# The w_down products of a hybrid mLSTM and attention block: factors without accumulating loads, gated factors split ahead, two-bank products

## The chip, the cores and the metric

One Trainium2 chip, one of its cores. The metric is the device time of one execution in microseconds: the median of several executions without the profiler. A profile is one further execution, taken with the profiler on; its own time stands beside its span below.

## What is computed

One block of a streaming encoder on 512 tokens of width 2048 in float32. A shared pre-normalised input feeds an mLSTM part and a differential attention part; their heads go through w_out and are added to x. The rest is a SwiGLU mixer, and this is the part that matters here:

```python
h2 = rmsnorm(x, norm2_g)                                   # 512 x 2048
x = x + (silu(h2 @ w_gate) * (h2 @ w_up)) @ w_down         # 5632 gated features
return rmsnorm(x, final_g)
```

w_gate and w_up are 2048 x 5632, w_down is 5632 x 2048. Every factor of a product is held as two numbers, hi (the value rounded to the matmul's format, `fp32r`) and lo (what is left), and each product is three matmuls: hi*hi, hi*lo and lo*hi.

## The kernel before

**Order of the stages.** In-projections, attention and mLSTM (to about 640 us of the profiled execution), w_out (to about 810 us), w_gate and w_up (810 to 1693 us), the w_down products (1693 to 2044 us), then a tail with what is left of w_down, the final norm and the stores.

**Gate and up.** `NFB` = 22 groups `g` of 256 features. Each runs `group` (L961) twice, for w_gate and then for w_up. A group multiplies by a block scheme with 7 products instead of 8 (names P1 to P7, in the order of `ORDER`), each product being 24 matmuls of 128x256 columns. Its weight factors come from the generator `left_factors` (L851), which loads blocks with SP, forms sums of blocks on DVE and splits each factor (`split`, L96: the hi cast on ACT at L98, the lo subtraction on DVE at L99). `factor` (L921) pulls factors `LAP` = 2 ahead of the product that uses them; whi and wlo have three buffers. `after` (L974) takes a product out of PSUM. At the end of the second group `up` (L1032) has the two gated tiles `C1` and `C2`. For g < 16 it forms seven combinations of their halves and POOL stores them to a DRAM tensor `actv`, in float32; for the last six groups POOL stores the tiles to `actd`.

**The w_down products (L1069).** The first 16 groups' rows of w_down are done in four row blocks (`ci`, 0 to 3) and two column halves (`dg`, 0 and 1), eight units `u` in all; each unit has seven products, in the order `DOWN`, and each product has 24 matmuls of 512 columns in two halves `h`. A product has three inputs:

- The weight factor. `load` (L885) fetches blocks of w_down with SP; for two of the five blocks of each `h` a second block is added in flight by an accumulating DMA that POOL issues (L891). Two more sums per `h` are formed on DVE (L913, L915). `upto` (L898) sets how many loads are issued ahead. The factor is then split at L98 and L99.
- The gated factor. `variant` (L946) loads one of the seven combinations for row block `ci` from `actv` with SP into a tile `ra` of two buffers (L952) and splits it on ACT and DVE into hi and lo tiles of the pool `A` (32 tiles). In the loop this happens during dg = 1, one variant per product, for the next row block; four are made in the last up group and three in unit 0.
- The sum so far. Each product is made anew in two PSUM banks (one of the pool `acc`, one of `aux`, four each), copied to a tile M by ACT in row block 0 (L1088), and added to M by DVE in the others (L1090), 512 columns at a time.

**The tail.** `combine` (L1097) turns the seven M tiles of a column half into blocks of the result on DVE, scales them on ACT, and POOL adds x1 from DRAM to them with an accumulating DMA. The last six feature groups are done in two chunks of four and two (`CHUNKS`) by `proj_tok` and the loop at L1212; `Gated` (L1125) loads and splits their activations, `last_weights` (L1166) loads and splits the last chunk's weights.

**What sets the order.** Each engine and each issuing queue (SP, POOL) works in its own fixed order and waits at the head of it. A planner puts the instructions into these orders when the kernel is built, following the program and tile reuse: a tile is given out again when its last reader is done, and the first writer of the new tile waits for that. So the SP queue stops at a load whose tile is still read, and ACT stops at a cast whose input has not landed.

Of the kernel before, what the change touches and what calls it, by code (L numbers as in the profile page):

```python
# [30 lines left out]
def build(nc, tc, ctx, a, out):  # L31
# [11 lines left out]
    pacc = pool("acc", 4, space=bass.MemoryType.PSUM)  # L43
    paux = pool("aux", 4, space=bass.MemoryType.PSUM)
# [23 lines left out]
    def tacc():  # L68
        return pacc.tile([128, 512], F32, tag="acc", name=nm("acc"))

    def taux():
        return paux.tile([128, 512], F32, tag="aux", name=nm("aux"))
# [763 lines left out]
    actd = dram.tile([NFB, 2, 128, 512], F32, name="actd")  # L836
    actv = dram.tile([4 * NSP, 7, 128, 256], F32, name="actv")
# [7 lines left out]
    DOWN = ["P1", "P3", "P6", "P5", "P7", "P4", "P2"]  # L845
# [5 lines left out]
    def left_factors():  # L851
# [33 lines left out]
        def load(u, h, i, ring):  # L885
            j, n, j2, n2 = ((0, 0, 0, 0), (1, 1, 1, 1), (0, 0, 0, 1), (1, 1, 0, 1), (1, 0, 1, 0))[i]
            ci, dg = divmod(u, 2)
            t = ring()
            nc.sync.dma_start(t, a["w_ds"][ci, dg, j, n, h])
            if (j, n) != (j2, n2):  # L890
                G.dma_start(t, a["w_ds"][ci, dg, j2, n2, h], accum_op=ALU.add)  # L891
            return t

        order = [(u, i, h) for u in range(2 * NSP) for i in range(5) for h in range(2)]
# [3 lines left out]
        def upto(k):  # L898
            while pos[0] < min(k, len(order)):
                u, i, h = order[pos[0]]  # L900
                got[u, i, h] = load(u, h, i, tR if h and (u, i) != (0, 0) else lambda: tW("raw", bufs=7))
                pos[0] += 1

        upto(2)
        for u in range(2 * NSP):
            k = 10 * u
            for pi, name in enumerate(DOWN):
                if u or pi:
                    upto(k + (14 if pi == 0 else 16 if pi < 6 else 20))
                for h in range(2):  # L910
                    B11, B22, T1, T3, B21 = (got.get((u, i, h)) for i in range(5))
                    if name == "P6":
                        V.tensor_tensor(B22, B22, T1, ALU.add)  # L913
                    if name == "P4":
                        V.tensor_tensor(B22, B22, B21, ALU.add)  # L915
                    yield parts({"P1": B11, "P3": B22, "P6": B22, "P5": T1, "P7": T3, "P4": B22, "P2": B21}[name])
# [28 lines left out]

    def variant(ci, name, into):  # L946

        v = ["P1", "P7", "P2", "P4", "P5", "P6", "P3"].index(name)
        into[name] = []
        for h in range(2):  # L950
            if more:
                r = more[2].tile([128, 512], F32, tag="ra", name=nm("ra"), bufs=2)  # L952
            else:
                r = tW("raw", bufs=7)[:, 0:512]
            g0 = 4 * ci + 2 * h
            nc.sync.dma_start(r.rearrange("p (g c) -> p g c", g=2), actv[g0:g0 + 2, v].rearrange("g p c -> p g c"))
            hi, lo = tA(), tA()
            split(hi, lo, r)
            into[name].append((hi, lo))

    def group(scale, done, first=False, last=False):  # L961
# [12 lines left out]
        def after(name):  # L974
            if name == "P1":
# [48 lines left out]
    for g in range(NFB):  # L1024
# [7 lines left out]
        def up(i, t):  # L1032
            V.tensor_tensor(t, t, sl[i], ALU.mult)
            if g >= 4 * NSP:
                G.dma_start(actd[g, i], t)
                return
# [10 lines left out]
            for k, t in ((0, C1), (2, C2), (4, Sa)):  # L1047
                G.dma_start(actv[g, k:k + 2].rearrange("v p c -> p v c"), t.rearrange("p (v c) -> p v c", v=2))
            G.dma_start(actv[g, 6], Sb[:, L])

        group(None, gate, first=g == 0)
        group(None, up, last=g == NFB - 1)


    late[0].close()
    mst, (pM,) = stage(("mm", 1),)
    more.extend(stage(("rr", 1), ("ra", 1)))
    more[1:] = more[1]
    M = [{}, {}]

    def product_down(banks, w, name, h):
        for m in range(2):
            rs = slice(m * 512, m * 512 + 512)
            hi, lo = got_v[name][h]
            for tt in range(2):
                ts = slice(m * 256 + tt * 128, m * 256 + tt * 128 + 128)
                three(banks[tt], hi[:, ts], lo[:, ts], w[0][:, rs], w[1][:, rs], h == 0 and m == 0, h == 1 and m == 1)

    for u in range(2 * NSP):  # L1069
        ci, dg = divmod(u, 2)  # L1070
        got_v = cur_v
        if dg == 1:
            cur_v = {}
        for pi, name in enumerate(DOWN):
            if u == 0 and pi < 3:
                variant(0, DOWN[4 + pi], cur_v)
            if dg == 1 and ci + 1 < NSP:
                variant(ci + 1, name, cur_v)
            banks = [tacc(), taux()]
            for h in range(2):  # L1080
                product_down(banks, factor(), name, h)
            if ci == 0:
                M[dg][name] = pM.tile([128, 1024], F32, tag="M", name=nm("M"), bufs=14)
            t = M[dg][name]
            for tt in range(2):
                cs = slice(tt * 512, tt * 512 + 512)
                if ci == 0:
                    SC.copy(t[:, cs], banks[tt])  # L1088
                else:
                    V.tensor_tensor(t[:, cs], banks[tt], t[:, cs], ALU.add)  # L1090

    more[0].close()
# [4 lines left out]
    def combine(dg):  # L1097
# [12 lines left out]
        V.tensor_tensor(P6, P6, P1, ALU.add)  # L1110
        V.tensor_tensor(P7, P7, P6, ALU.add)
        V.tensor_tensor(P4, P4, P7, ALU.add)
        out_(P4, 1, 0)
        V.tensor_tensor(P3, P3, P5, ALU.add)
        V.tensor_tensor(P3, P3, P6, ALU.subtract)
        out_(P3, 0, 1)
# [210 lines left out]
```

## Time and profile before

| | us |
|---|---|
| median of 3 executions | 2181.36 |
| lowest and highest of them | 2181.03, 2182.97 |
| the profiled execution, its own time | 2190.05 |
| its span, first to last instruction | 2188.3 |
| span after the start of the w_down products | 495.1 |

The page of the profile gives each engine's busy time over the span; the stretches in the rows below give the same by stage. PE is TensorE's matmuls, PEld its weight loads, DVE VectorE, ACT ScalarE, POOL GpSimd, SP the queue that issues most DMAs. PEclk is the share of full clock that TensorE was granted: 1.00 is 2.4 GHz, 0.50 is 1.2 GHz. A matmul's printed duration covers its whole passage and is longer than the step from one to the next, so work is counted by the step between starts. Idle time stands in brackets behind an instruction with what ended it.

### The profile page before, as it was taken

How to read it: one execution, taken by the hardware profiler on the slowest of the kernel's cores; microseconds unless marked ns; L12 is line 12 of the kernel's file. 1: busy time of each engine (PE TensorE's matmuls, PEld its weight loads, DVE VectorE, ACT ScalarE, POOL GpSimd, SP SyncE). 2: the span in 40 equal slices, each digit the busy share in tenths (PEclk: the TensorE clock that was granted, in tenths of full speed). 3: DMA queues.
4: the chain of work that ended last, by engine and by line, in shares of the span. 5: the costliest groups of instructions: out<-in, count | busy, mean ns of one | idle time of the engine just before them, and what ended most of it. 6: DMA issues, size and time to landing. Idle time of an engine off the chain costs nothing.

```text
span 2188.3 us, 33437 instructions
## 1 busy us (share of the span) xinstructions
PE 2142.0 (98%) x13305; PEld 1938.2 (89%) x13305; DVE 1569.6 (72%) x2362; ACT 992.7 (45%) x1515; POOL 133.8 (6%) x189
## 2 busy tenths in 40 slices
PE   9999999999999999999999999999999799999998
PEld 7888889988888889999999999999999577778786
DVE  6267776366544468888888888888889467779745
ACT  6256675355434354344344443343444454444423
POOL 0011110000000000000000000000000000001100
PEclk9999999999999999999999999999999999999999
DMA  6232112332234424343443434433335986876732
GB/s 257 96 96 78 62 53 72 116 97 87 82 112 146 140 92 131 124 145 119 129 135 119 137 121 133 131 123 117 121 121 168 284 228 184 242 210 156 203 106 77
DMA packets 100749, 292.56 MB, mean 134 GB/s; under 512 B 10976, under 2 KB 27376, under 8 KB 100592
## 3 DMA queue, kind: packets, MB, share of 16 engines
q1 hardware_dynamic: 86832, 247.42, 34.5%
q0 software_dynamic: 13760, 43.00, 8.4%
q8 instruction: 104, 1.70, 0.3%
q14 instruction: 53, 0.43, 0.1%
HBM read 264.16 MB, written 26.22 MB: 133 GB/s over the span
## 4 chain that ended last, share of the span: by engine, by line
PE 85%; DMA 6%; DVE 6%; ACT 2%; issue 1%; ACTq 0%; POOL 0%; DVEq 0%; SPq 0%; POOLq 0%
PE acc L159 9%; PE acc L158 9%; PE acc L160 9%; PE acc L933 8%; PE acc L932 8%; PE acc L931 8%; PE aux L933 6%; PE aux L932 6%; PE aux L931 6%; DMA ra<-actv 4%; PE acc L189 4%; PE acc L190 4%; PE acc L191 4%; DVE wlo L99 2%; PE aux L160 1%
## 5 line engine op out<-in xcount | busy, mean ns | idle before, releaser
L98 ACT CAST whi<-raw 128x1024 fp32r<-128x1024 f32 (+2 forms) x573 | 593.6, 1037 | 807.4 <-PE acc L932 238.8
L99 DVE TENSOR_TENSOR wlo<-raw,whi 128x1024 fp32r<-128x1024 f32 (+2 forms) x573 | 690.5, 1206 | 305.8 <-ACT whi L98 295.0
L158 PE MATMUL acc<-whi,A 128*128 128x512 f32 (+1 forms) x1056 | 404.0, 384 | 21.4 <-ACT whi L98 18.2
L159 PE MATMUL acc<-wlo,A 128*128 128x512 f32 (+1 forms) x1056 | 403.7, 382 | 9.5 <-DVE wlo L99 9.5
L160 PE MATMUL acc<-whi,A 128*128 128x512 f32 (+1 forms) x1056 | 400.7, 379 | 0.0
L158 PEld LDWEIGHTS acc<-whi,A 128*128 128x128 f32 x1056 | 200.0, 190 | 59.4 <-ACT whi L98 22.5
L159 PEld LDWEIGHTS acc<-wlo,A 128*128 128x128 f32 x1056 | 200.3, 190 | 48.0 <-DVE wlo L99 15.0
L160 PEld LDWEIGHTS acc<-whi,A 128*128 128x128 f32 x1056 | 200.4, 190 | 34.0
L932 PE MATMUL acc<-A,whi 128*128 128x256 f32 x704 | 199.3, 283 | 0.5 <-DVE A L99 0.5
L931 PE MATMUL acc<-A,whi 128*128 128x256 f32 x704 | 199.4, 283 | 0.0
L931 PE MATMUL acc<-h,whi 128*128 128x256 f32 x704 | 199.4, 283 | 0.0
L933 PE MATMUL acc<-h,wlo 128*128 128x256 f32 x704 | 199.2, 283 | 0.0
L932 PE MATMUL acc<-h,whi 128*128 128x256 f32 x704 | 199.2, 283 | 0.0
L933 PE MATMUL acc<-A,wlo 128*128 128x256 f32 x704 | 199.2, 283 | 0.0
L933 PE MATMUL aux<-h,wlo 128*128 128x256 f32 x528 | 149.7, 284 | 0.8 <-DVE wlo L99 0.8
L931 PE MATMUL aux<-h,whi 128*128 128x256 f32 x528 | 149.6, 283 | 0.6 <-ACT whi L98 0.6
L189 PE MATMUL acc<-A,whi 128*128 128x512 f32 x384 | 150.1, 391 | 0.0
L190 PE MATMUL acc<-A,whi 128*128 128x512 f32 x384 | 149.8, 390 | 0.0
L191 PE MATMUL acc<-A,wlo 128*128 128x512 f32 x384 | 149.8, 390 | 0.0
L933 PE MATMUL aux<-A,wlo 128*128 128x256 f32 x528 | 149.4, 283 | 0.0
L931 PE MATMUL aux<-A,whi 128*128 128x256 f32 x528 | 149.4, 283 | 0.0
L932 PE MATMUL aux<-A,whi 128*128 128x256 f32 x528 | 149.4, 283 | 0.0
(280 smaller groups left out, 4123.9 us busy)
## 6 DMA issues: line engine op xcount, KB each, us to landing
raw<-in_w_g_dram SPq DMA_DIRECT2D x88, 512.0 KB, 3.5
raw<-in_w_u_dram SPq DMA_DIRECT2D x88, 512.0 KB, 3.6
raw<-in_w_ds_dram SPq DMA_DIRECT2D x80, 512.0 KB, 5.1
raw<-in_w_aqk_dram SPq DMA_DIRECT2D x32, 512.0 KB, 3.4
raw<-in_w_o_dram SPq DMA_DIRECT2D x32, 512.0 KB, 3.5
raw<-in_w_ds_dram POOLq DMA_DIRECT2D x32, 512.0 KB, 8.2
raw<-in_w_b_dram SPq DMA_DIRECT2D x31, 512.0 KB, 4.0
actv<-x POOLq DMA_DIRECT2D x48, 256.0 KB, 3.4
```

What stands on the lines that cost most here:

```text
L98: SC.copy(hi, src)
L99: V.tensor_tensor(lo, src, hi.bitcast(F32), ALU.subtract)
L158: PE.matmul(acc, lh, rh, start=first, stop=False)
L159: PE.matmul(acc, lh, rl, start=False, stop=False)
L160: PE.matmul(acc, ll, rh, start=False, stop=last)
L189: PE.matmul(banks[f], wh[:, cs], xh[k], start=first, stop=False)
L190: PE.matmul(banks[f], wh[:, cs], xl[k], start=False, stop=False)
L191: PE.matmul(banks[f], wl[:, cs], xh[k], start=False, stop=last)
L931: PE.matmul(bank, w[0][:, cs], hi, start=m == 0, stop=False)
L932: PE.matmul(bank, w[0][:, cs], lo, start=False, stop=False)
L933: PE.matmul(bank, w[1][:, cs], hi, start=False, stop=m == 7)
```

## The change

Four things are changed, all in or around the w_down products.

1. *Weight factors.* The block scheme's order is now P1, P5, P3, P7, P2, P6, P4, and each unit loads its four blocks per `h` once, all with SP. The accumulating DMAs are gone; the four sums per `h` that the scheme needs are formed on DVE in place.
2. *Gated factors.* They are split where they are made. `up` queues calls (`later`) that split each tile, hi into a new tile x and lo in place, and POOL stores both halves; `after` runs one of them behind the products P1, P6, P7 and P2 of the next group. `variant` then is four loads per product straight into hi and lo tiles, with no work on ACT or DVE. The pool of these tiles grows from 32 to 38 (`tAA`), and the table `NEXT` says at which product of which half the next row block's variants are loaded. The last six groups' activations (`actd`, `Gated`) are treated likewise, and the first chunk of them takes the place of a fifth row block in `NEXT`.
3. *PSUM.* Until the end of gate and up it is `acc` and `aux` as before. In the w_down products P1 of each column half has two banks of its own and gathers all four row blocks there, never copied to M; the other six products share two pairs of banks, and are taken out by one instruction over 1024 columns. In the tail `acc` has four banks where the pairs were.
4. *Tail.* `combine` is a generator in four steps, one at each of the first two granules of every column block; `last_weights` yields once more, between a load and its splits.

```diff
+    def tAA():
+        nAA[0] += 1
+        if (nAA[0] - 1) % 38 < 32:
+            return tA()
+        return more_a[0].tile([128, 512], F32R, tag="aa", name=nm("aa"))
...
-        def load(u, h, i, ring):
-            j, n, j2, n2 = ((0, 0, 0, 0), (1, 1, 1, 1), (0, 0, 0, 1), (1, 1, 0, 1), (1, 0, 1, 0))[i]
-            ci, dg = divmod(u, 2)
-            t = ring()
-            nc.sync.dma_start(t, a["w_ds"][ci, dg, j, n, h])
-            if (j, n) != (j2, n2):
-                G.dma_start(t, a["w_ds"][ci, dg, j2, n2, h], accum_op=ALU.add)
+        def load(u, i, h):
+            j, n = ((0, 0), (0, 1), (1, 1), (1, 0))[i]
+            t = tR() if (h if u else i > 1) else tW("raw", bufs=7)
+            nc.sync.dma_start(t, a["w_ds"][u // 2, u % 2, j, n, h])
...
-        upto(2)
+        upto(4)
...
-                    upto(k + (14 if pi == 0 else 16 if pi < 6 else 20))
+                    upto(8 * u + (8, 8, 8, 10, 10, 12, 14)[pi])
...
+                    t, o = {"P1": (B11, None), "P5": (B11, B12), "P3": (B22, None), "P7": (B12, B22),
+                            "P2": (B21, None), "P6": (B11, B22), "P4": (B21, B11)}[name]
+                    if o is not None:
+                        V.tensor_tensor(t, t, o, ALU.add)
+                    yield parts(t)
...
     def variant(ci, name, into):
...
-            nc.sync.dma_start(r.rearrange("p (g c) -> p g c", g=2), actv[g0:g0 + 2, v].rearrange("g p c -> p g c"))
-            hi, lo = tA(), tA()
-            split(hi, lo, r)
-            into[name].append((hi, lo))
+            into[name].append((tAA(), tAA()))
+            for p in range(2):
+                nc.sync.dma_start(into[name][h][p].bitcast(F32), actv[p, v, 2 * ci + h])
...
         def after(name):
+            if later and name in ("P1", "P6", "P7", "P2"):
+                later.pop(0)()
...
+            def halves(t):
+                hi, lo = tX(F32R)[:, :t.shape[1]], t.bitcast(F32R)
+                split(hi, lo, t)
+                return hi, lo
...
+            def keep(k, t, g=g, cs=cs):
+                for p, r in enumerate(halves(t)):
+                    r = r.bitcast(F32)
+                    if k == 6:
+                        G.dma_start(actv[p, 6, g // 2, :, cs], r)
+                    else:
+                        G.dma_start(actv[p, k:k + 2, g // 2, :, cs].rearrange("v p c -> p v c"),
+                                    r.rearrange("p (v c) -> p v c", v=2))
+            later.extend(partial(keep, k, t) for k, t in ((0, C1), (2, C2), (4, Sa), (6, Sb[:, L])))
...
+    psum[0].close()
+    pst, (pP1,) = banks_of(("p1", 2))
+    psum[:] = banks_of(("pair", 2))
+    NEXT = {(0, 3): 0, (0, 5): 1, (1, 1): 2, (1, 2): 3, (1, 3): 4, (1, 4): 5, (1, 5): 6}
...
+            nxt = NEXT.get((dg, pi))
+            if nxt is not None:
+                if ci + 1 < NSP:
+                    variant(ci + 1, DOWN[nxt], cur_v[1])
+                elif nxt < CHUNKS[0]:
+                    chunks[0].more(tAA)
+            if name == "P1":
+                if ci == 0:
+                    M[dg][name] = pP1.tile([128, 1024], F32, tag="p1", name=nm("p1"))
+                bank, fresh_, done_ = M[dg][name], ci == 0, ci == NSP - 1
+            else:
+                bank, fresh_, done_ = psum[1][0].tile([128, 1024], F32, tag="pair", name=nm("pair")), True, True
...
-                if ci == 0:
-                    SC.copy(t[:, cs], banks[tt])
-                else:
-                    V.tensor_tensor(t[:, cs], banks[tt], t[:, cs], ALU.add)
+                SC.copy(M[dg][name], bank)
+            else:
+                V.tensor_tensor(M[dg][name], bank, M[dg][name], ALU.add)
```

## Rows read from the trace of the kernel before

**Rows 1.** The page, section 1: PE's busy time, share, instructions.

```profile
PE 2142.0 (98%) x13305; PEld 1938.2 (89%) x13305; DVE 1569.6 (72%) x2362; ACT 992.7 (45%) x1515; POOL 133.8 (6%) x189
```

**Rows 2.** By stretch: length, busy us PE, PEld, DVE, ACT, POOL; PEclk, DMA.

```profile
850.00:1650.00 800.00, 800.00 (x6669) 800.00 (x6668) 693.00 (x857) 325.94 (x358) 46.95 (x71) 1.00 0.40 127
1693.24:1800.00 106.76, 89.79 (x357) 70.20 (x356) 59.45 (x61) 55.35 (x78) 11.42 (x14) 0.92 0.90 263
1800.00:2000.00 200.00, 189.19 (x799) 153.30 (x798) 161.67 (x183) 85.61 (x96) 17.88 (x21) 0.97 0.75 205
2000.00:2043.60 43.60, 43.60 (x194) 36.10 (x193) 43.59 (x50) 24.01 (x30) 5.20 (x6) 1.00 0.57 151
2043.60:2178.80 135.20, 132.60 (x577) 109.06 (x575) 73.47 (x109) 47.01 (x82) 6.93 (x8) 0.99 0.40 123
```

**Rows 3.** Groups by line and shape, from 1650 us to the end, PE.

```profile
L158 PE MATMUL acc<-whi,A 128*128 128x512 f32 x352 | 141.2, 401 | 20.9 <-ACT whi L98 18.2 <-DVE M L1186 2.6
L158 PE MATMUL aux<-whi,A 128*128 128x512 f32 x224 | 89.4, 399 | 0.0
L158 PE MATMUL acc<-A,b 128*128 128x512 f32 x52 | 20.2, 389 | 0.0
L158 PE MATMUL acc<-b,b 128*128 128x512 f32 x12 | 4.7, 389 | 0.0
```

**Rows 4.** Timeline of PE: start, duration, instruction.

```profile
1693.24 0.40 PE L158 MATMUL acc<-whi,A 128*128 128x512 f32 x1
...
2171.62 0.39 PE L160 MATMUL acc<-A,b 128*128 128x512 f32 x1
...
2178.42 0.39 PE L160 MATMUL acc<-A,b 128*128 128x512 f32 x1
```

**Rows 5.** Timeline of PE: three of the 18 matmuls with idle time before them.

```profile
1714.83 0.80 PE L158 MATMUL acc<-whi,A 128*128 128x512 f32 x1 [5.45 <-ACT whi L98]
...
1958.22 0.78 PE L158 MATMUL acc<-whi,A 128*128 128x512 f32 x1 [3.00 <-ACT whi L98]
...
2070.84 0.77 PE L158 MATMUL acc<-whi,A 128*128 128x512 f32 x1 [2.60 <-DVE M L1186]
```

**Rows 6.** Waits from 1690 us on: who waited for whom, us, times, longest.

```profile
ACT A L98 <- DMA ra<-actv: 69.4, 31, 6.2
```

**Rows 7.** Groups by line and shape in the w_down products, DVE.

```profile
L99 DVE TENSOR_TENSOR wlo<-raw,whi 128x1024 fp32r<-128x1024 f32 x113 | 137.6, 1221 | 31.3 <-ACT whi L98 31.0
L99 DVE TENSOR_TENSOR A<-ra,A 128x512 fp32r<-128x512 f32 x46 | 31.6, 688 | 40.3 <-ACT A L98 40.0
L1090 DVE TENSOR_TENSOR M<-acc,M 128x512 f32<-128x512 f32 x41 | 28.1, 684 | 0.5 <-PE acc L160 0.3
L913 DVE TENSOR_TENSOR raw<-raw,raw 128x1024 f32<-128x1024 f32 x16 | 19.5, 1222 | 12.0 <-DMA raw<-in_w_ds_dram 11.8
```

**Rows 8.** Timeline of one weight factor of w_gate/w_up: ACT, DVE, PE.

```profile
1207.44 1.05 ACT L98 CAST whi<-raw 128x1024 fp32r<-128x1024 f32 x1 [2.63 <-DVE raw L873]
...
1208.53 1.23 DVE L99 TENSOR_TENSOR wlo<-raw,whi 128x1024 fp32r<-128x1024 f32 x1
...
1212.28 0.28 PE L931 MATMUL aux<-h,whi 128*128 128x256 f32 x1
```

**Rows 9.** DMA from 1690 to 2100 us: queues (packets, MB, share); issues (KB, us).

```profile
q1 hardware_dynamic: 28168, 66.29, 47.2%
q0 software_dynamic: 7072, 21.50, 29.1%
...
ra<-actv SPq DMA_DIRECT2D x46, 256.0 KB, 4.4
```

**Rows 10.** The chain that ended last, 1690 to 1735 us: start, duration, what.

```profile
1699.82 19.27 DMA ra<-actv
```

**Rows 11.** Who issues DMAs: SP's loads of actv; POOL's stores of actv.

```profile
L956 SPq DMA_DIRECT2D ra<-actv x48: 359/377/378, 895.4 to 1960.1; - x48
...
L1048 POOL DMA_DIRECT2D actv<-x x47 | 33.5, 713 | 567.7 <-DVE x L1033 509.2 <-DVE x L1046 54.7 <-DVE x L1044 3.6
```

## What the change is predicted to do

> **What bounds the kernel now.** The page comes first: PE is busy for 2142 of 2188.3 us [rows 1], so only a stage where PE stands still can give anything, unless the change takes matmuls away. It takes none away: the w_down products have 8 units x 7 products x 24 matmuls = 1344 before and after, the tail 384 + 192. The second view is the busy time by stretch [rows 2]. From 850 to 1650 us, in gate and up, PE is busy for 800 of 800 us at full clock: nothing can be won there, only lost. In the w_down products PE is busy for 89.8 of the first 106.8 us and 189.2 of the next 200, at a granted clock of 0.92 and 0.97; the last 43.6 us of them are full; the tail lacks 2.6 us.
>
> What is that worth? From the first w_down matmul at 1693.24 to the last of the kernel at 2178.42 us [rows 4] there are 640 calls of `three`: 352 + 224 + 52 + 12 [rows 3], so 1920 matmuls. Their undisturbed step comes from the end of the trace: 30 steps of PE's program lie between 2171.62 and 2178.42 us [rows 4], which is 0.2267 us each. 1920 of them take 435.3 us; the trace took 2178.42 + 0.23 - 1693.24 = 485.4. So 50.1 us are lost. The same sum by stretch, matmuls counted against length / 0.2267: (471 - 356) x 0.2267 = 26 us in the first 107 us, 19 in the next 200, none until 2043.6, 4.4 in the tail [rows 2]. A second way gives the same: the 18 bracketed idle times on PE sum to 30.3 us (as the stretches do: 17.0 + 10.8 + 2.6 [rows 2]); each costs about 0.16 more, because the printed 0.39 us of a matmul is longer than its step [rows 4], so 3; and the granted clock was low for the equivalent of 0.08 x 106.8 + 0.03 x 200 + 0.01 x 135 = 16 us [rows 2]. Behind the longer stops the steps are those of the lower of the two levels, 1.2 GHz: the first matmul after 5.45, 3.00 and 2.60 us of idle took 0.80, 0.78 and 0.77 us instead of 0.39 [rows 5, 4]. So a stop costs about half as much again as its length.
>
> What ends the stops? Always a late whi or wlo, or in the tail a late evacuation [rows 5]. Behind it stands ACT: it waited 69.4 us in 31 waits for `ra<-actv` [rows 6], and while it waits, the weight cast behind it in its queue stands too; DVE waits 40.0 us in turn [rows 7]. The load of a variant into `ra` comes late because only two `ra` tiles exist. The other source, at the start, is the burst of loads: DMA share 0.90 over the first 107 us [rows 2], and one 256 KB load took 19.27 us to land [rows 10] where the median is 4.4 [rows 9].
>
> **The change part by part.**
>
> *Gated factors, in the w_down products.* 56 casts and 56 subtractions of 512 columns leave ACT and DVE; on DVE that is 56 x 0.688 = 38.5 us [rows 7]. More important, neither queue has anything left that waits for `actv`: only PE's own weight loads wait for it. The variants of the next row block now go straight into hi and lo tiles. With 38 tiles and 28 in use, two variants fit ahead, and the later ones are issued one product after the product that frees their tiles. Each is issued seven or eight products, about 7 x 24 x 0.2267 = 38 us, before it is used; the worst landing seen is 19.27 us [rows 10]. Hence no wait on PE from there. Cost: 56 more issues on SP of 0.377 us [rows 11], 21 us in 305, and what stands behind each in SP's queue: the weight loads, when SP waits for PE to free a tile. These are issued four or more products (22 us) ahead of use. I cost it at nothing; the cover is that lead, and without it the price is the second rival below.
>
> *Weight factors.* The 32 accumulating DMAs go. The two queues' rates are 66.29 MB in 47.2% and 21.50 MB in 29.1% of 410 us [rows 9], so 343 and 180 GB/s at full share: the POOL queue's bytes were nearly twice as dear. Two units (one row block) move 16 x 0.524 + 28 x 0.262 = 15.7 MB instead of 28 x 0.524 + 14 x 0.262 = 18.3 MB, 8 of the 28 accumulating. 15.7 MB at 343 GB/s are 46 us of the 76 us that two units take on PE. DVE does 32 more sums of 1024 columns: 32 x 1.222 = 39.1 us [rows 7], beside PE.
>
> *Two-bank evacuation.* The trace shows no 1024-column read of PSUM. Nearest rows: the same sum over 512 columns takes 0.684, over 1024 columns in SBUF 1.222 us [rows 7]; two of the first are 1.37, so between 1.2 and 1.4. I take 1.22, the row with the same length. P1 is not taken out at all: 36 x 1.22 = 44 us replace 84 x 0.684 = 57 us in row blocks 1 to 3. DVE over the products changes by -38.5 + 39.1 - 57 + 44 = -13 us. A pair is given out again two products later, so an evacuation may be up to 5.4 us late. In four of seven products DVE has two sums, two subtractions and one evacuation, 5 x 1.22 = 6.1 us against 5.44 of PE; at most two of these follow each other, 1.3 us in excess, and the other three need 2.4 to 3.7 us. Price 0, bounds 0 and 3 us in all.
>
> *Splits in gate and up.* Per group g < 16 three splits of 512 and one of 256 columns, per later group two of 512: DVE gets 3 x 0.688 + 0.42 = 2.5 us [rows 7] (the 256 taken as 0.6 of the 512), ACT 3.5 x 0.53 = 1.9 us (half of the cast over 1024 columns each [rows 8]; ACT is busy for 326 of 800 us [rows 2]), POOL four more stores of 0.713 us [rows 11]. A pair of groups takes 2 x 7 x 24 matmuls of 800 / 6669 = 0.12 us [rows 2], 40.3 us; DVE is busy for 693 of 800 us [rows 2], 34.9 per pair, so 37.4 after. It stays below PE. Is the depth enough? The latest factor in the pair that I followed: its cast starts at 1207.44 because a sum on DVE was late, its lo is done at 1208.53 + 1.23 = 1209.76, and PE starts that product at 1212.28 [rows 8]: 2.5 us to spare. One split of 0.69 us per product fits. Price 0, bounds 0 and 20 us (1 us per pair).
>
> *Start of the products.* This stays partly. Unit 0 needs 4.2 MB of variants (four of seven; three come earlier), 4.2 MB of weights and the last 1 MB of `actd` stores, 9.4 MB, then 5.2 MB of loads ahead. At 263 / 0.90 = 292 GB/s [rows 2] the 9.4 MB take 32 us and unit 0 takes 38 on PE. But they stand in one queue, and B22, wanted by the third product at 1704, is issued behind three or four variants of 1.05 MB (3.6 us each) and four weight blocks, some 17 to 19 us after 1685, to which a cast and a subtraction of 2.3 us [rows 8] come. So between 0 and 14 us of stop with its clock; I take 4, near the lower end, because every load before it is efficient, where the row's 19.27 us stood behind accumulating DMAs.
>
> *Tail.* No split of `actd` is left there, chunk 0 is loaded during the last row block, and a load of last weights now has a granule of time before its split, so that DVE's evacuation no longer stands behind it: the 4.4 us of the tail go. P1 from PSUM in `combine` costs what it did. Another 2 us I leave for stops that I don't see.
>
> Sum against the profiled execution: 2190.05 - 50.1 + 4 + 2 = 2146. The median of the runs is 8.7 us below the profiled execution. If that is a constant of profiling, the result is 2137; if it lies in the same waits that go, 2146. Nothing in one trace tells; I take the middle, 2142.
>
> **The rivals.**
>
> *The queue decides (second likeliest).* Variants in two halves double the bytes that stand in front of the weight loads. For it: the 19.27 us of a 256 KB load [rows 10]. Against: outside the start the need is 46 us of 76. Price: unit 0's whole 14.7 MB at 292 GB/s takes 50 us against 38, so 12 us plus half for the clock, 18 at the start, and 5 later: 23 in place of 6, so 2159. The Trainium skill (DMA: Bandwidth & Descriptors, Queues, rings and completion order) states that each engine consumes a ring's descriptors in ring order; by that rule a load waits for all that its queue issued before. The row of 19.27 us agrees with it.
>
> *DVE waits in gate and up (slower).* The new lo waits for a hi that stands on ACT behind a weight cast, and that cast waits for PE; DVE's queue stands meanwhile. The place is the first group of each pair; it decides from 40.3 - 37.4 = 2.9 us of such waits per pair. If each of four splits costs half of one cast and its wait, (2.63 + 1.05) / 2 = 1.8 us [rows 8], that is 7.4 per pair, 4.5 beyond the slack, 16 x 4.5 = 72 us lost for 48 won (with two splits in the last six groups inside the slack): 2142 + 72 = 2214. Half of the excess still gives 2178. Against: 2.5 us to spare on the worst factor, and the splits stand right behind a product's end, when ACT's cast has just been released.
>
> *The wait only moves (no change).* PE waits itself for what ACT waited for, if the planner issues the variants later than their place in the program: 2181, up or down by some 10. For it: transfers double in number, and each landed in 4.4 us at the median. The Trainium skill (DMA: Bandwidth & Descriptors, Anatomy of one DMA) gives a fixed cost of some 2 us to a transfer, which speaks against halving them; by its figures 256 KB would take an estimated 2.6 us. The trace's median is above that, and what counts is the lead, not the landing.
>
> **How the numbers follow.** Forecast 2142: 0.68. Queue, 2159: 0.17. DVE, 2178 to 2214: 0.08. Only moved, about 2181: 0.07. Low end: all 50.1 us gone and 8.7 constant, 2131, so 2130. High end: the queue's case with the unscaled profile, 2163, and 10 of the 20 us that bound gate and up: 2173. Outside lie DVE, the moved wait and a little of the first, under 0.2. About 0.2% (4.4 us) can be told from no change. Faster: 0.68 + 0.17 + 0.02 = 0.87; same 0.04; slower 0.09.
>
> **What would show it.** In the profile after: no `ACT A <- DMA ra` and no accumulating DMA before the tail; PE busy for over 98% of 1693 to 2044 us's counterpart, that stage 305 to 315 us long instead of 350; gate and up still 800 of 800 with DVE near 92%; the tail at 135 - 4 us. I am wrong if PE shows idle time in gate and up, if `PE <- DMA A<-actv` waits appear row block after row block, or if the start loses its 26 us again.

## The result, and the profile after

| | before | after |
|---|---|---|
| median of 4 runs each, us | 2182.16 | 2149.88 |
| lowest and highest | 2181.03, 2185.79 | 2149.33, 2150.66 |
| the profiled execution, its own time | 2190.05 | 2149.33 |
| its span | 2188.3 | 2147.6 |
| first w_down matmul to the end of the last matmul | 485.4 | 443.0 |

The changed kernel is faster: the ratio is 0.9849, with a 95% interval of 0.9832 to 0.9867. The medians differ by 32.3 us; 39.4 had been forecast. Against the 435.3 us that 1920 undisturbed matmuls take [rows 3, 4], the trace of after loses 443.0 - 435.3 = 7.7 us, where before lost 50.1.

Where they are lost is seen by stretch, in the same columns as [rows 2] (length, busy us of PE, PEld, DVE, ACT, POOL, then clock, DMA share and GB/s):

```profile
850.00:1650.00 800.00, 800.00 (x6669) 800.00 (x6669) 727.26 (x930) 359.12 (x430) 94.98 (x144) 1.00 0.46 149
1695.06:1800.00 104.94, 104.94 (x463) 86.92 (x464) 77.90 (x68) 51.63 (x52) 1.49 (x3) 1.00 0.75 270
1800.00:2000.00 200.00, 200.00 (x884) 165.59 (x883) 177.48 (x153) 83.75 (x85) 8.14 (x10) 1.00 0.59 186
2000.00:2137.80 137.80, 131.39 (x575) 107.34 (x574) 72.01 (x104) 42.69 (x75) 5.69 (x7) 1.00 0.41 127
```

Gate and up are as full as before, with DVE at 727 us instead of 693. The w_down products are full from the first matmul to the last: 104.94 us hold 463 matmuls, which is what 104.94 / 0.2267 gives, and the clock is 1.00. All that is lost lies in the tail, where 137.8 us would hold 608 and held 575. PE's timeline shows the same; these are all matmuls of the w_down part that had idle time before them, the first being the change of stage, the other four in the tail:

```profile
1695.06 0.47 PE L164 MATMUL p<-whi,A 128*128 128x512 f32 x1 [1.00 <-issue]
...
2003.04 0.50 PE L164 MATMUL acc<-whi,aa 128*128 128x512 f32 x1 [1.73 <-DVE M L1148]
...
2024.76 0.47 PE L164 MATMUL acc<-whi,aa 128*128 128x512 f32 x1 [1.03 <-DVE M L1224]
...
2031.08 0.50 PE L164 MATMUL acc<-whi,aa 128*128 128x512 f32 x1 [3.34 <-DVE M L1224]
...
2053.58 0.50 PE L164 MATMUL acc<-whi,aa 128*128 128x512 f32 x1 [0.31 <-DVE M L1224]
```

Each of the four waits for an evacuation, as [rows 5] showed one of 2.60 us in the tail of before. Why DVE was late is read one engine further back. This is the timeline of ACT and DVE before the longest stop (start, duration, instruction, idle time and what ended it):

```profile
2029.02 1.14 ACT L104 CAST A<-raw 128x512 fp32r<-128x512 f32 x2 [6.33 <-DMA raw<-in_w_d_dram]
2029.67 0.69 DVE L105 TENSOR_TENSOR A<-raw,A 128x512 fp32r<-128x512 f32 x1 [4.40 <-ACT A L104]
...
2030.28 0.74 DVE L1224 SCALAR_TENSOR_TENSOR M<-acc,rstd,M 128x512 f32<-128x512 f32 x1
```

ACT stood 6.33 us at the cast of a last weight that had not landed, DVE stood 4.40 us at the subtraction behind it, and the evacuation (L1224) stood behind that in DVE's queue. The chain of waits says what that load waited for. It goes round: a load is issued when a split on DVE gives its `raw` tile back, and the split stands behind the load before it (start, duration, what).

```profile
2011.01 1.15 DVE wlo L105
2012.15 0.02 issue
2012.17 7.79 DMA raw<-in_w_d_dram
...
2021.77 0.70 DVE A L105
2022.47 0.02 issue
2022.49 6.51 DMA raw<-in_w_d_dram
```

The DMA view from 1690 to 2100 us, as [rows 9] (packets, MB, share of 16 engines; then count, KB and median us from issue to landing):

```profile
q1 hardware_dynamic: 29605, 76.43, 53.8%
q0 software_dynamic: 2624, 5.24, 7.1%
...
raw<-in_w_ds_dram SPq DMA_DIRECT2D x60, 512.0 KB, 5.1
A<-actv SPq DMA_DIRECT2D x75, 256.0 KB, 3.9
...
aa<-actv SPq DMA_DIRECT2D x16, 256.0 KB, 4.4
...
M<-x1d POOLq DMA_DIRECT2D x16, 256.0 KB, 6.2
```

The 5.24 MB that are left on POOL's queue are x1's accumulating loads (16 x 0.262) and four `actd` stores. They still go at 5.24 MB / (0.071 x 410 us) = 180 GB/s, the rate of before.

### The profile page after: what moved, and what is told of

It is laid out like the page before. It is cut to its first block, busy times and chain, and to the rows that moved or that the text cites. A ratio compares the mean times of both kernels' runs of the same rounds, so it can differ in the third digit from the quotient of the medians.

```text
span 2147.6 us, 33652 instructions
## 1 busy us (share of the span) xinstructions
PE 2123.6 (99%) x13305; PEld 1929.1 (90%) x13305; DVE 1591.2 (74%) x2354; ACT 989.4 (46%) x1507; POOL 156.3 (7%) x233
## 4 chain that ended last, share of the span: by engine, by line
PE 93%; DVE 2%; DMA 2%; ACT 1%; issue 1%; SPq 0%; ACTq 0%; DVEq 0%
PE acc L165 8%; PE acc L164 8%; PE acc L166 8%; PE acc L935 8%; PE acc L934 8%; PE acc L933 8%; PE aux L935 6%; PE aux L934 6%; PE aux L933 6%; PE pair L164 4%; PE pair L165 4%; PE pair L166 4%; PE acc L195 4%; PE acc L196 4%; PE acc L197 4%; DMA raw<-in_w_d_dram 2%
## 5 line engine op out<-in xcount | busy, mean ns | idle before, releaser
L164 PE MATMUL acc<-whi,A 128*128 128x512 f32 (+1 forms) x816 | 306.4, 377 | 1.3 <-ACT whi L104 0.8
L165 PE MATMUL acc<-wlo,A 128*128 128x512 f32 (+1 forms) x816 | 305.0, 374 | 0.0
L166 PE MATMUL acc<-whi,A 128*128 128x512 f32 (+1 forms) x816 | 304.4, 373 | 0.0
L164 PEld LDWEIGHTS acc<-whi,A 128*128 128x128 f32 x816 | 153.1, 188 | 25.7 <-ACT whi L104 1.5
L166 PEld LDWEIGHTS acc<-whi,A 128*128 128x128 f32 x816 | 153.2, 188 | 24.6
L165 PEld LDWEIGHTS acc<-wlo,A 128*128 128x128 f32 x816 | 153.3, 188 | 24.2 <-DVE wlo L105 0.6
```

The costliest lines, as they stand in the source:

```text
L164: PE.matmul(acc, lh, rh, start=first, stop=False)
L165: PE.matmul(acc, lh, rl, start=False, stop=False)
L166: PE.matmul(acc, ll, rh, start=False, stop=last)
```

## The experiments

The runs are compared with the kernel before by the ratio of their medians; "lost" is the length from the first w_down matmul to the end of the last in that run's trace, less 435.3 us.

| run | median (range), us | ratio (95%) | lost, us |
|---|---|---|---|
| before | 2182.16 (2181.03 to 2185.79) | 1 | 50.1 |
| after | 2149.88 (2149.33 to 2150.66) | 0.9849 (0.9832 to 0.9867) | 7.7 |
| b_noacc | 2151.04 (2149.21 to 2152.08) | 0.9857 (0.9837 to 0.9877) | 11.3 |
| a_accum | 2163.8 (2163.36 to 2164.97) | 0.9917 (0.9898 to 0.9937) | 22.9 |
| a_late2 | 2154.02 (2153.25 to 2156.21) | 0.9873 (0.9854 to 0.9893) | 12.0 |
| b_ra3 | 2166.72 (2164.94 to 2169.28) | 0.9933 (0.9909 to 0.9958) | 25.2 |
| b_noacc_ra3 | 2150.52 (2147.85 to 2152.91) | 0.9843 (0.9828 to 0.9858) | 12.3 |
| b_plain | 2157.6 (2156.72 to 2160.9) | 0.9882 (0.9866 to 0.9898) | 18.2 |
| a_lead1 | 2150.54 (2149.48 to 2151.21) | 0.9837 (0.9822 to 0.9851) | 10.4 |
| a_dve1 | 2157.38 (2156.72 to 2158.73) | 0.9869 (0.9854 to 0.9884) | 8.8 |
| a_dve2 | 2159.98 (2159.83 to 2160.15) | 0.9881 (0.9864 to 0.9897) | 7.2 |
| a_tail | 2151.12 (2149.76 to 2151.48) | 0.9839 (0.9824 to 0.9853) | 8.5 |
| a_tailold | 2150.26 (2149.39 to 2151.8) | 0.9846 (0.9832 to 0.9861) | 8.3 |
| a_plainx | 2143.58 (2143.27 to 2144.38) | 0.9818 (0.9805 to 0.9832) | 1.9 |

### Which part gives the gain

**Part 1 alone (b_noacc):** the kernel before with plain loads of the weight blocks, their sums on DVE and the new order of the products (the loads are shown).

```diff
...
-            t = ring()
-            nc.sync.dma_start(t, a["w_ds"][ci, dg, j, n, h])
-            if (j, n) != (j2, n2):
-                G.dma_start(t, a["w_ds"][ci, dg, j2, n2, h], accum_op=ALU.add)
+            t = tR() if (h if u else i > 1) else tW("raw", bufs=7)
+            nc.sync.dma_start(t, a["w_ds"][u // 2, u % 2, j, n, h])
...
```

> The kernel before with one part of the change: four blocks per half, no accumulating DMA, four sums on DVE, the new order of products. Theory A: casts of variants still stand in front of weight casts, 2170 to 2180. Theory B: most of the gain, 2150 to 2162.

2151.04 us: within 1.2 us of the whole change, whose interval its own overlaps. Theory A, on which the prediction stood, falls. The variants still have two `ra` tiles and ACT still waits for them, 23 times; this is the row of b_noacc that answers to [rows 6]:

```profile
ACT A L98 <- DMA ra<-actv: 32.3, 23, 2.8
```

The waits are shorter, 2.8 us at the longest instead of 6.2; b_noacc_ra3 below shows that without them the kernel takes the same time.

**Part 1 undone (a_accum):** the changed kernel with the accumulating loads and the old order of the products; the diff is the one above, read the other way.

> The changed kernel with the weight factors of the kernel before: five blocks per half, two of them with a second block added by an accumulating DMA that POOL issues, two sums on DVE, the old order of products. Everything else stays changed. Theory A (the 32 us came from ACT and DVE no longer waiting for variants): the loads that accumulate are still far enough ahead, so at most 10 us are lost, 2150 to 2160. Theory B (the accumulating loads filled the DMA engines and were late themselves): 20 us or more are lost, 2170 or above.

2163.8 us, between the two: 13.9 us of the 32 are lost, so with accumulating loads there the other parts still bring 18. The loss is at the start; from 1800 to 2000 us PE is full, and the tail loses 9.3 us, not much more than after. The stretches of a_accum:

```profile
1693.24:1800.00 106.76, 97.19 (x409) 79.10 (x409) 58.50 (x51) 47.13 (x47) 13.74 (x18) 0.95 1.05 341
1800.00:2000.00 200.00, 200.00 (x884) 165.68 (x883) 156.06 (x132) 81.06 (x79) 19.03 (x23) 1.00 0.87 264
```

The DMA engines are busy without a gap at the start (the share of 1.05 is full) and 62 of 471 matmuls don't come to run until 1800, 14 us. The variants' doubled bytes show here: their loads land after 7.7 us at the median, where they take 3.9 after (without accumulating loads) and 4.4 before (with them, and with half the bytes).

**Part 2 undone (a_late2):** gated factors stored once in float32, loaded into two `ra` tiles and split in the products (the loads are shown; the pool of hi and lo tiles has 36 tiles, not 38, and the last six groups go back likewise).

```diff
...
-            into[name].append((tAA(), tAA()))
-            for p in range(2):
-                nc.sync.dma_start(into[name][h][p].bitcast(F32), actv[p, v, 2 * ci + h])
...
+                r = more[2].tile([128, 512], F32, tag="ra", name=nm("ra"), bufs=2)
...
+            nc.sync.dma_start(r, actv[0, v, 2 * ci + h])
+            hi, lo = tAA(), tAA()
+            split(hi, lo, r)
+            into[name].append((hi, lo))
...
```

> The changed kernel with the gated factors as in the kernel before: stored in float32, loaded into two tiles ra and split on ACT and DVE inside the products (36 instead of 38 tiles A, to make room); the weight factors, the two-bank products and the tail stay changed. Theory A: ACT stands again at casts whose load has not landed, and most of the gain goes: 2170 to 2182. Theory B: without accumulating DMAs the loads are early enough, at most 10 us are lost: 2150 to 2160. On DVE the gate and up stage falls back from about 91% to 87% either way.

2154.02 us, so B. The step that the prediction held for the more important is worth 4 us once the accumulating loads are gone. PE runs 883 matmuls from 1800 to 2000 us, as many as after, although DVE is busy for 193.7 of the 200; most of what is lost more lies in the tail.

**A third `ra` tile in the kernel before (b_ra3),** `bufs=2` to `bufs=3`, nothing else.

> The kernel before with three tiles ra instead of two and nothing else changed. If the number of these tiles makes the variants late (the first cause that the prediction names), a third of the lateness goes and 8 to 15 us with it: 2167 to 2174. If the loads are late for another reason (full DMA engines, their place in SP's queue), nothing changes: 2178 to 2184.

2166.72 us: 15 us for one tile of 256 KB. So the prediction's cause was one, but not the only one: with the loads mended nearly all of the lost time goes, with the tiles mended half of it (25.2 us are left of 50.1).

**Both together in the kernel before (b_noacc_ra3).**

> The kernel before with plain loads and sums of the weight blocks (the change's part 1 alone) and three tiles for the variants instead of two. Theory 1 (two causes that overlap: the loads, and the count of tiles): the 23 waits of ScalarE for variants, 32 us in the kernel with part 1 alone, go almost wholly, and with them some 6 us of stops in the row blocks: 2143 to 2147 us. Theory 2 (the waits that are left fit into the slack, and the stops come from elsewhere): the waits go and the time stays, 2149 to 2152 us.

2150.52 us: theory 2. ACT's waits for variants are down to 3.0 us in 2, and the time is that of b_noacc: from 1800 to 2000 us PE runs 871 matmuls instead of 861, and the tail takes that back. Three stops are left in its row blocks, of 1.05, 1.00 and 1.00 us, each at a lo that DVE gave late:

```profile
1706.61 0.50 PE L159 MATMUL acc<-wlo,A 128*128 128x512 f32 x1 [1.05 <-DVE wlo L99]
...
1844.06 0.50 PE L159 MATMUL acc<-wlo,A 128*128 128x512 f32 x1 [1.00 <-DVE wlo L99]
...
1921.72 0.50 PE L159 MATMUL acc<-wlo,A 128*128 128x512 f32 x1 [1.00 <-DVE wlo L99]
```

DVE is busy there for 195 of 200 us (1800 to 2000), with the sums of part 1 on it and the splits and single-bank evacuations still there. In the changed kernel it is busy for 177.5 and the stops are gone. The splits are not what makes them: a_late2 has the splits, a DVE that is busy for 193.7 us, and no stop there. What it shares with the changed kernel is part 3, more tiles for the variants and earlier places for their loads; which of these ends the stops was not tried. Beside part 1, all the rest of the change is worth some 6.6 us of products: b_noacc loses 6.7 us there and 4.7 in the tail, the changed kernel 0.1 and 7.7. Only 1.2 us of it are left in the medians, because the tail loses more and the products start 1.25 us later (1695.06 against 1693.81).

### What is dear about an accumulating load

**The same loads without the addition (b_plain):** in the kernel before, at L891.

```diff
-                G.dma_start(t, a["w_ds"][ci, dg, j2, n2, h], accum_op=ALU.add)
+                G.dma_start(t, a["w_ds"][ci, dg, j2, n2, h])
```

> The kernel before; its 32 loads that accumulate on landing (B22 and B21 onto the first block, for T1 and T3) are issued as plain loads of the same bytes, on the same queue, with the same waits. What it leaves out: the addition, so the factors T1 and T3 lack their first block. Theory 1 (the read, add and write of an accumulating load is what is dear): the rate of that queue rises towards the other's and the loads land sooner, so most of the 31 us that the loads' removal gave comes here too: 2150 to 2163 us. Theory 2 (two loads for one factor, one after the other, and the bytes are what is dear): nothing changes in either, 2175 to 2184 us. In between: both have a share, in the proportion of the time.

2157.6 us: the addition on landing costs 25.4 us, against the 2182.95 of the runs of before beside it. The second load in series, the bytes, POOL's order and the order of the products share the 6.6 that lie between this and b_noacc; they were not taken apart. The queues of b_plain from 1690 to 2100 us:

```profile
q1 hardware_dynamic: 28798, 68.55, 49.5%
q0 software_dynamic: 7072, 21.50, 18.7%
...
raw<-in_w_ds_dram POOLq DMA_DIRECT2D x32, 512.0 KB, 6.8
```

Against [rows 9]: the same 21.50 MB in the same 7072 packets take 18.7% of the engines' time instead of 29.1. What else is on that queue, x1's loads above all, takes 6.3% in b_noacc; without it, the 32 loads of 0.524 MB go at 16.8 MB / (0.124 x 410 us) = 330 GB/s at full share instead of 16.8 / (0.228 x 410) = 180. The landing falls from 8.2 us (before, same view) to 6.8, and ACT's waits for variants, which are on the other queue, from 69.4 to 43.5. It is the long landings that shrink: those of the variants' loads have a median of 4.4 us before and 4.2 here, but the longest falls from 19.3 us to 13.7.

### How much lead the variants need

**One product instead of seven or eight (a_lead1):** each variant of row blocks 1 to 3 is placed in the program of the changed kernel one product ahead of its use.

```diff
-    NEXT = {(0, 3): 0, (0, 5): 1, (1, 1): 2, (1, 2): 3, (1, 3): 4, (1, 4): 5, (1, 5): 6}
+    NEXT = {(1, 6): 0}
...
+            if ci > 0 and dg == 0 and pi < 6:
+                variant(ci, DOWN[pi + 1], got_v)
...
```

> The changed kernel with the variants of row blocks 1 to 3 loaded inside their own block, each placed in the program one product before it is used, instead of seven or eight. If the long lead is what hides the doubled transfers: stops at many products, 10 us or more, above 2160. If the loads fit one product of 5.44 us (their median landing is 3.9 us) or the SP queue runs ahead of its place in the program anyway: at most 3 us, 2149 to 2153.

2150.54 us, no change, and no stop in the products. But the lead did not get shorter, which was the second of the two reasons given for the lower expectation: SP runs ahead of the loads' place in the program. The first row is a_lead1's loads of variants into the six added tiles (first and last start), the second the changed kernel's, the third a_lead1's first matmul of row block 3:

```profile
L964 SPq DMA_DIRECT2D aa<-actv x16: 320/378/802, 1727.6 to 1910.5; - x16
```

```profile
L964 SPq DMA_DIRECT2D aa<-actv x16: 319/327/414, 1708.1 to 1910.4; - x16
```

```profile
1922.77 0.39 PE L164 MATMUL p<-whi,A 128*128 128x512 f32 x1
```

The last of these loads is the last variant of row block 3. It starts at 1910.5 in both kernels, 12 us before that row block does and 45 us before its product (the seventh, at 1955.41). How short a lead the kernel would bear was therefore not tested.

### What reserve gate and up have

**One or two needless sums of 512 columns on DVE for each new split (a_dve1, a_dve2).**

```diff
             def halves(t):
+                for _ in range(1):
+                    V.tensor_tensor(junk, bc2, bc2, ALU.add)
```

> The changed kernel with one more DVE sum of 512 columns per split in gate and up (four per pair of groups for g < 16, two after; its result is used by nobody). The changed kernel's DVE is busy for 37.5 of 40.3 us in such a pair; 4 x 0.6 makes it 39.9. The prediction's slack of 2.9 us says that nothing is lost: 2149 to 2152. If DVE's waits for ACT already use the slack: 1 us per pair or more, 2160 or above.

> The changed kernel with two such sums per split: 8 x 0.6 = 4.8 us per pair, 42.3 of 40.3. DVE now is the bound in 16 of 22 pairs: at least 16 x 2.0 = 32 us are lost, 2180 or above, and gate and up shows idle time on PE. If the added sums hide in DVE's bracketed idle time more than by this count: 2155 to 2175.

2157.38 and 2159.98 us: the first between its two expectations, the second inside the lower one, 7.5 and 10.1 us above the median of after. But the planner did not spread the sums as the program has them: in a_dve1 all 76, of 0.68 us each, run before 1203 us, 69 of them after 850. The stretches before and after 1203 us, first of a_dve1, then of a_dve2, then of the changed kernel:

```profile
850.00:1203.00 353.00, 351.88 (x2897) 348.39 (x2897) 351.20 (x485) 155.32 (x193) 48.49 (x72) 1.00 0.48 153
1203.00:1500.00 297.00, 297.00 (x2477) 297.00 (x2476) 274.01 (x355) 133.36 (x161) 38.49 (x58) 1.00 0.46 150
```

```profile
850.00:1203.00 353.00, 351.51 (x2894) 347.94 (x2893) 350.54 (x485) 155.09 (x193) 48.48 (x72) 1.00 0.47 153
1203.00:1500.00 297.00, 296.06 (x2440) 293.21 (x2439) 295.38 (x406) 128.67 (x158) 37.71 (x56) 1.00 0.46 149
```

```profile
850.00:1203.00 353.00, 353.00 (x2944) 353.00 (x2944) 324.53 (x423) 160.61 (x195) 48.55 (x72) 1.00 0.48 155
1203.00:1500.00 297.00, 297.00 (x2478) 297.00 (x2477) 272.34 (x352) 133.97 (x162) 39.93 (x60) 1.00 0.47 151
```

In a_dve1 some 47 us of sums meet 28.5 us that DVE has free in the first stretch. It is busy there for 99.5%, and PE lacks 47 matmuls, 47 x 0.12 = 5.6 us; in the second stretch, with DVE busy for 92%, PE runs 2477 where the changed kernel runs 2478. With two sums per split DVE is at 99% in both, PE lacks 50 and 38 matmuls, and the w_down products start at 1706.07, 11 us late. So the rival by which DVE waits in gate and up had the right place and the wrong price: a DVE without any time left costs 10 us in all and not 30 or 70. The added sums wait for nothing; work that waits for ACT, as the rival had it, was not tried, nor were sums that stay spread over the pairs, as a_dve1 was meant to have them.

### What stops the tail

**Last weights one piece earlier (a_tail).**

```diff
...
+        fetch(0)
+        for i in range(4 * CHUNKS[-1]):
+            fetch(i + 1)
+            yield
+            r = got.pop(0)
...
```

> The changed kernel with one change in the tail: each load of last weights is issued one piece earlier, so two loads are in flight and a load has two granules (10.9 us) instead of one (5.4 us) before its splits. Theory T (in the tail ACT stands at splits whose load takes 6.5 us to land, DVE behind it, and the evacuation of a product behind that on DVE): the stops of 1.03, 3.34 and 0.31 us in the tail go with their clock, 4 to 7 us, 2143 to 2146. Rival (the evacuation waits for x1, which the accumulating DMAs of combine bring late): no change, 2148 to 2151.

2151.12 us; the theory fell. ACT still stands at casts whose load has not landed, for 7.1 us at the longest, and the loads in the chain of waits take 4.17, 6.30 and 7.15 us: the splits came forward along with the loads.

**The tail's order of before (a_tailold)** in the changed kernel: `combine` at one go, load and split of a last weight together.

```diff
...
-    steps = chain(combine(0), combine(1))
+    for _ in combine(0):
+        pass
...
+            if n > 0 and g % 2 == 1 and (n, g) != (3, 3):
+                next(wait, None)
...
```

> The changed kernel with the order of the tail as it was: both combinations at one go, and load and split of the last weights together at every second granule. Theory 1 (the tail's stops come from the new order, which splits the last weights early and spreads the accumulating loads of the input): the stops of 1.7, 1.0 and 3.3 us become those of before (2.6 us in all), 2144 to 2148 us. Theory 2 (they come from the arrival of the last weights and of the input, which is the same in both orders): 2149 to 2152 us.

2150.26 us: theory 2. Its two stops in the tail are 1.59 and 4.19 us. Part 4 of the change is worth nothing that can be measured, in either direction.

**x1's loads without the addition (a_plainx),** at L1166 of the changed kernel.

```diff
-                G.dma_start(x1[tt][2 * dg + n], x1d[tt, 2 * dg + n], accum_op=ALU.add)
+                G.dma_start(x1[tt][2 * dg + n], x1d[tt, 2 * dg + n])
```

> The changed kernel; the 16 loads that add the input x onto the combined products in the tail are issued as plain loads of the same bytes, on the same queue with the same waits. What it leaves out: the addition, so the input replaces the first part of the result. Theory 1 (these accumulating loads hold up the last weights, whose late arrival stands behind the tail's three stops of 1.73, 1.03 and 3.34 us): the median landing of the x loads falls from 7.5 us to 4 to 5, the waits of ScalarE for last weights in the 50 us around the stops fall from 22 us to under 12, and most of the 7.7 us go: 2142 to 2146 us. Theory 2 (the last weights are late because each load waits for one of seven tiles that the split behind it frees): the landing falls, but the stops and the time stay, 2148 to 2151 us.

2143.58 us: theory 1. The tail now loses next to nothing. The queue and the loads of a_plainx from 1690 to 2100 us, then ACT's waits for last weights from 1690 us on (22.2 after):

```profile
q0 software_dynamic: 1600, 5.24, 3.8%
...
M<-x1d POOLq DMA_DIRECT2D x16, 256.0 KB, 3.4
```

```profile
ACT A L104 <- DMA raw<-in_w_d_dram: 16.3, 5, 5.0
```

The same 5.24 MB take 3.8% instead of 7.1, so 336 GB/s instead of 180, and the landing falls from 6.2 us to 3.4. The waits shrink by less than expected (a quarter, not half), but of the stops behind them only this is left beside the change of stage:

```profile
2002.04 0.50 PE L164 MATMUL acc<-whi,aa 128*128 128x512 f32 x1 [1.02 <-DVE M L1148]
```

So in the changed kernel the ring of last weights becomes a stop of PE when the accumulating loads share the DMA engines with it. Those loads alone don't make the stop: b_ra3 and b_plain have them too, and their tails are nearly full. These are their stretches from the first matmul of the tail to the end of the last, with 576 matmuls to run and one that was already running:

```profile
2021.93:2153.88 131.95, 130.87 (x577) 107.87 (x575) 73.58 (x109) 47.23 (x82) 6.93 (x8) 1.00 0.41 126
```

```profile
2015.28:2146.99 131.71, 130.86 (x577) 107.84 (x575) 73.27 (x109) 46.94 (x82) 6.93 (x8) 1.00 0.40 126
```

They lose 131.95 - 576 x 0.2267 = 1.4 us and 1.1 us, where after loses 7.7. What else it takes is open. A kernel that adds x1 in another way and keeps the result was not run; where its tiles would lie is open. No kernel that keeps the whole computation came out measurably below the changed one.

## Why the prediction was right, and where not

The direction and the range held; the forecast was 7.9 us too low, some 4 by halving the 8.7 us and 3.5 by start and tail together (1.8 + 7.7 measured, 4 + 2 forecast). By its steps:

- **What bounds the kernel, and that 50.1 us are lost:** held. 42.4 of them went.
- **The cause.** The step that failed. The prediction took the wait that the trace names most, `ra<-actv` with 69.4 us, and the two tiles behind it for the cause, and the burst of loads for a second one at the start. In the kernel before the tiles are a cause: a third one gives 15 us. But part 1 alone gives 31 us and leaves 32 us of that wait; part 2 undone costs 4. That the total held all the same is partly luck: the change took both causes away, and the sum did not depend on which of them held the 50.1 us. The row of the wait told who stood, not why the load was late. The figure that pointed to it was in the prediction: 343 against 180 GB/s. It was used to count bytes; b_plain shows that these loads also hold up those of the variants on the other queue.
- **Weight factors, 32 more sums on DVE at price 0:** right for the whole change, where the price is 0. Alone they bring DVE to 193 of 200 us and PE to 861 of 882 matmuls (b_noacc, 1800 to 2000), 871 where a third `ra` tile takes ACT's waits for variants away.
- **Two-bank evacuation, estimated at 1.22 us:** right. The group of the changed kernel, 1690 to 2000 us:

```profile
L1148 DVE TENSOR_TENSOR M<-pair,M 128x1024 f32<-128x1024 f32 x35 | 42.8, 1222 | 7.0 <-PE pair L166 6.5
```

- **Splits in gate and up, price 0:** right. DVE is busy for 727.26 of 800 us, 36.6 per pair of groups where 37.4 was forecast, and PE for all 800.
- **Start of the products, 4 us:** measured 1.8, the shift of the first matmul (1693.24 to 1695.06), of which 1.0 is the idle time in front of it and the rest lies earlier. The mis-sized term is the rate: 292 GB/s was a rate with accumulating loads in it. In after, the 40 us from 1690 on moved 15.65 MB, 391 GB/s. Nothing came late.
- **Tail, 4.4 us go:** wrong, 7.7 are lost. It was argued from DVE's order; the loads that accumulate there were not costed, and they were left as they are by the change. 2 us had been left for what isn't seen. Of the terms of the sum it has the largest error, 5.7 us.
- **The 8.7 us between profile and median:** mis-sized too. Halved, it made 2146 into 2142. Later profiles lie within 2.4 us of their medians in every run, and runs of before spread from 2177.9 to 2189.7; so the profile of before was a long draw, not a constant on top. The measured parts add up: 2190.05 - 50.1 + 1.8 + 7.7 = 2149.4, where the profiled execution of after took 2149.33.
- **The rivals.** The queue doesn't decide after the change. In a_accum, where the doubled variants meet the accumulating loads, 14 us go at the start, for which 18 had been worked out; but the kernel before lost 26 there with accumulating loads and single variants, so the doubled bytes are not shown to be the cause. DVE in gate and up was refuted for the change, and a_dve2 shows that a DVE with no time left there costs 10 us. The wait did not move to PE: no stop in the products waits for `A<-actv`; how much of the lead that takes is open, since a_lead1 did not shorten it. The Trainium skill's figures (DMA: Bandwidth & Descriptors, Anatomy of one DMA) made an estimated 2.6 us for a load of 256 KB; the page fits them to DMAs that GpSimd issues. The plain loads of that size on GpSimd's queue here, x1's in a_plainx, land after 3.4 us at the median, and the variants of the changed kernel on SP's after 3.9 and 4.4.

## What to carry to other kernels

When the trace says that an engine waits for a load, look at what else is on the DMA engines before blaming the number of tiles: divide MB by share for each queue, and a queue with half the rate of the other is the suspect for every late load, on other queues too. Two causes that overlap don't add: mending one gave 31 us here, mending the other 15, both 32. A wait that is longer in total than another need not be the one that decides: here 32 us of it, in waits of 2.8 us at the longest, cost nothing. And look in the trace whether an edit did what it says: a planner that reorders can leave a load where it was (a_lead1) or gather what was meant to be spread (a_dve1).

## What the runs showed that was not expected

- A load that adds on landing takes the DMA engines' time nearly twice over: 180 GB/s at full share, against 330 (w_down's, b_plain) and 336 (x1's, a_plainx) for the same bytes on the same queue as plain loads. It slows loads on the other queue: ACT's waits for variants fell from 69.4 to 43.5 us with nothing of theirs changed, their loads' longest landing from 19.3 to 13.7 us.
- The share that DVE is busy does not tell alone what it costs PE. At 92% of a stretch (a_dve1, 1203 to 1500 us) and at 97% (a_late2, 193.7 of 200 us) PE lost nothing; at 97.5% (b_noacc_ra3, 195 of 200) it had two stops of 1.00 us; at 99.5% (a_dve1, 850 to 1203 us) it lacked 47 of 2944 matmuls.
